# Loading four more input pieces before the first output store of a store-bound kernel

## The chip, the cores and the metric

The kernel runs on one core of one Trainium2 chip. The metric is the time of one execution on the device in microseconds (us), the median of several runs. The engines are named as in the profile. In that of the kernel before, PE runs the matrix products and transposes (2304 instructions), DVE, ACT and POOL the copies and casts (384, 481 and 106, a few other instructions of ACT and POOL among them), SP and ACT issue the transfers, and the DMA engines, of which the profile counts sixteen, carry them. SBUF and PSUM are the two memories that the program places its tiles in. Kernels are compared only within the same rounds.

## The reference

```python
# q, k: 8 x 12 x 1024 x 64, float32
def reference(q, k):
    return np.einsum('bhid,bhjd->bhij', q, k).astype(np.float32)
```

These are 96 heads. Each takes 256 KB of q and 256 KB of k and gives a 1024 x 1024 float32 matrix of 4 MB. In all 50.33 MB are read and 402.65 MB are written.

## The kernel before

Blocks of heads go through these steps: a load of raw float32 pieces (four pieces a block: q and k, twice), a cast to float16 on POOL, a transpose on PE, a copy to SBUF on DVE, the score matmuls on PE, copies of eight 128 x 1024 tiles a head from PSUM on ACT (tiles 0, 2, 3, 5, 7) and DVE (tiles 1, 4, 6), and one store of 4 MB a head, issued by SP. Blocks 0 and 1 have two heads, all others four. The parts that matter here:

```python
in_pool = ctx.enter_context(tc.tile_pool(name="in_pool", bufs=8))    # raw pieces, 512 KB each
out_pool = ctx.enter_context(tc.tile_pool(name="out_pool", bufs=4))  # 4 MB each
...
    def scores(self, n, side):
        ...
        for t in range(NT):
            ps = po_pool.tile([P, S], F32, tag="po")      # three PSUM buffers
            ...                                           # two matmuls
            if t in (1, 4, 6):
                pin(nc.vector.tensor_copy(out=o_sb[:, t], in_=ps))
            else:
                pin(nc.scalar.copy(out=o_sb[:, t], in_=ps))
            if t in side:
                side[t]()
        pin(nc.sync.dma_start(out=..., in_=o_sb))         # the store
...
# first loads: blocks 0 to 2 into a free output buffer ("early"), block 3 into in_pool
for b in blocks[:3]:
    for n in range(4):
        ...
        b.load(n, (nc.sync, nc.scalar)[n % 2], piece)
for n in range(4):
    blocks[3].load(n, (nc.sync, nc.scalar)[n % 2])
...
stream = [(b, n) for b in blocks[4:] for n in range(4)]
...
        b.scores(n, side)
        if i == n == 0:
            next_load()          # after head 0: a pair of loads on ACT's queue
        next_load()              # after every head: one load on ACT's queue
        if nxt and a == nxt.G - 1 and 0 < i + 3 < len(blocks):
            to_half(blocks[i + 3 : i + 4])   # casts
```

So four of the eight input buffers stay empty at the start, and the first of them are filled by the pair that follows head 0. Every instruction is kept in program order on its engine. ACT both copies tiles and issues loads, and it does so in that order.

Of the kernel before, what the change touches and what calls it, by code (L numbers as in the profile page):

```python
# [15 lines left out]
def kernel(  # L16
# [6 lines left out]
    nc = tc.nc  # L23
# [118 lines left out]
    blocks, first = [], 0  # L142
# [10 lines left out]
    for b in blocks[:3]:  # L153
# [1 line left out]
            piece = raw[:, at + n * b.elems :][:, : b.elems]  # L155
            b.load(n, (nc.sync, nc.scalar)[n % 2], piece)
        at += 4 * b.elems
    for n in range(4):
        blocks[3].load(n, (nc.sync, nc.scalar)[n % 2])
    make_identity(nc, ident)  # L160

    def to_half(some):
        half_sb = half_pool.tile([P, 2 * half_elems], F16, tag="half")
        at = 0
        for b in some:
            b.place(half_sb, at)
            at += 2 * b.elems
            for n in range(4):
                b.cast(n)

    to_half(blocks[:2])
    to_half(blocks[2:3])



    stream = [(b, n) for b in blocks[4:] for n in range(4)]

    def next_load():
        if stream:
            b, n = stream.pop(0)  # L180
            b.load(n, nc.scalar)

    blocks[0].alloc()
    for x in range(2):
# [1 line left out]
    for i, b in enumerate(blocks):  # L186
        nxt = blocks[i + 1] if i + 1 < len(blocks) else None
        if nxt:
            nxt.alloc()
        heads = 2 * b.G  # L190
        for n in range(heads):
            a = n - max(0, heads - 1 - nxt.G) if nxt else -1
            side = {}
            if nxt and 0 <= a < nxt.G:
                side = {
                    1: lambda: nxt.transpose(a, 0),
                    6: lambda: nxt.transpose(a, 1),
                }
            b.scores(n, side)
            if i == n == 0:  # L200
                next_load()
            next_load()
            if nxt and a == nxt.G - 1 and 0 < i + 3 < len(blocks):
                to_half(blocks[i + 3 : i + 4])


# [28 lines left out]
```

## Time and profile before

| | before |
|---|---|
| median of the first three runs | 1074.59 us |
| span of the profiled run | 1074.4 us |
| bytes moved by DMA | 453.42 MB, mean 422 GB/s |
| busy share of PE, ACT, DVE, POOL | 69%, 44%, 43%, 9% |
| chain that ended last | 79% DMA, stores landing |
| first store issued | 19.56 us |

The way to read it: the DMA engines are busy for 90% or more of every slice but the last, and they move 426 to 436 GB/s in every slice between the first and the last, while PE, the busiest compute engine, is between 40 and 90% in all but one of these (that one at 90% or more), so the time is the bytes over the rate, plus whatever time the DMA engines lose. I measure it with one figure, the **lag** at time t: t less the bytes moved until t over 431 GB/s. The bytes come from adding up the trace's packet records (a packet under way counts in proportion), so the lag is worked out and is not a view of the profile. It rises where the DMA engines stand idle or move less than 431 GB/s, and stays level where they run at that rate. It is a mean over the sixteen DMA engines. The prediction quotes the lines of before.

### The profile page before, as it was taken

Reading aid. Unit: us, or ns where it says so; the run is one execution under the profiler, and the core shown is the slowest. Engines: PE = TensorE matmul, PEld = TensorE weight load, DVE = VectorE, ACT = ScalarE, POOL = GpSimd, SP = SyncE. Lnnn points to the kernel's source line nnn. Section 1 sums busy time; section 2 is a strip of 40 time slices with the busy share of each in tenths; the row PEclk is TensorE's granted clock in tenths of the full one; section 3 lists DMA queues with packets and bytes.
Section 4 is the critical chain, followed back from the end, with each engine's and each line's share of the span. In section 5 each row is a group of like instructions: output and inputs, shape, how many; then the busy total and the mean of one; then the engine's idle time right before and its main releaser. Section 6 shows DMA issues by size and latency. Waiting matters only on the chain.

```text
span 1074.4 us, 6393 instructions
## 1 busy us (share of the span) xinstructions
PE 743.6 (69%) x2304; PEld 267.3 (25%) x2304; DVE 463.7 (43%) x384; ACT 477.2 (44%) x481; POOL 100.7 (9%) x106
## 2 busy tenths in 40 slices
PE   7977677676776757667676676767767676678740
PEld 2322222222222212222222222222222222223210
DVE  4645354452534535345353443434434444445420
ACT  4545444444444434444443544444444443544530
POOL 4100101010010100101010010100101010000000
PEclk9965555555555555555555555555555555555555
DMA  9999999999999999999999999999999999999993
GB/s 332 430 429 433 429 433 432 428 431 433 429 432 431 431 427 436 429 428 435 431 429 434 427 431 434 427 432 434 426 433 433 429 430 432 432 431 429 436 432 170
DMA packets 28257, 453.42 MB, mean 422 GB/s; under 512 B 3136, under 2 KB 3136, under 8 KB 15936
## 3 DMA queue, kind: packets, MB, share of 16 engines
q1 hardware_dynamic: 14976, 405.81, 87.7%
q10 hardware_dynamic: 13248, 47.19, 11.0%
q8 instruction: 18, 0.29, 0.1%
q14 instruction: 15, 0.12, 0.0%
HBM read 50.33 MB, written 402.65 MB: 422 GB/s over the span
## 4 chain that ended last, share of the span: by engine, by line
DMA 79%; PE 12%; ACT 4%; issue 0%; DVE 0%; ACTq 0%; POOL 0%; SPq 0%
DMA out_dram<-o_sb 79%; PE ps L128 12%; ACT o_sb L132 4%; PE t_ps L103 1%; DMA early<-in_q_dram 0%; DVE o_sb L130 0%; DVE kT L115 0%; ACTq L132 0%; POOL half_sb L88 0%; SPq L75 0%
## 5 line engine op out<-in xcount | busy, mean ns | idle before, releaser
L128 PE MATMUL ps<-kT,qT 64*128 64x512 f16 x1536 | 657.3, 621 | 289.8 <-ACT o_sb L132 286.4
L132 ACT COPY o_sb<-ps 128x1024 f32<-128x1024 f32 x480 | 475.9, 1013 | 554.7 <-DMA out_dram<-o_sb 347.6
L130 DVE COPY o_sb<-ps 128x1024 f32<-128x1024 f32 x288 | 352.7, 1225 | 568.9 <-DMA out_dram<-o_sb 404.5
L128 PEld LDWEIGHTS <-qT 64*128 64x128 f16 x1536 | 193.2, 134 | 687.0 <-issue 680.2
L88 POOL CAST half_sb<-x_sb 128x1024 f16<-128x1024 f32 x88 | 91.3, 1040 | 835.0 <-DMA x_sb<-in_k_dram 404.6
L103 PE MATMUL t_ps<-ident,half_sb 128*128 128x128 f16 x768 | 99.0, 310 | 6.1 <-POOL half_sb L88 6.1
L103 PEld LDWEIGHTS <-half_sb 128*128 128x128 f16 x768 | 74.1, 141 | 84.4 <-issue 62.4
L115 DVE COPY qT<-t_ps 128x1024 f16<-128x1024 f16 x48 | 60.6, 1263 | 7.2 <-PE t_ps L103 7.2
L115 DVE COPY kT<-t_ps 128x1024 f16<-128x1024 f16 x48 | 58.3, 1215 | 0.2 <-PE t_ps L103 0.2
L88 POOL CAST half_sb<-early 128x512 f16<-128x512 f32 (+1 forms) x12 | 8.7, 755 | 5.4 <-DMA early<-in_q_dram 5.4
L132 ACT ACT_TABLE_LOAD x1 | 1.3, 1283 | 8.8 <-DMA early<-in_q_dram 8.8
masks.py:199 POOL TENSOR_SCALAR_AFFINE_SELECT ident<-ident 128x128 f16<-128x128 f16 x1 | 0.3, 292 | 0.1
masks.py:197 POOL MEMSET ident<- 128x128 f16 x1 | 0.2, 204 | 0.3 <-POOLq L219 0.3
L219 POOL MEMSET const-float32-0.0<- 128x1 f32 x1 | 0.1, 98 | 0.2 <-issue 0.2
L219 POOL MEMSET const-bfloat16-1.0<- 128x1 bf16 x1 | 0.1, 101 | 0.0
L219 POOL MEMSET const-uint8-127<- 128x1 uint8 x1 | 0.1, 101 | 0.0
L219 POOL MEMSET const-float32-1.0<- 128x1 f32 x1 | 0.1, 98 | 0.0
## 6 DMA issues: line engine op xcount, KB each, us to landing
out_dram<-o_sb SPq DMA_DIRECT2D x96, 4096.0 KB, 36.7
x_sb<-in_k_dram ACTq DMA_DIRECT2D x44, 512.0 KB, 32.1
x_sb<-in_q_dram ACTq DMA_DIRECT2D x42, 512.0 KB, 32.1
early<-in_k_dram ACTq DMA_DIRECT2D x4, 256.0 KB, 5.0
early<-in_q_dram SPq DMA_DIRECT2D x4, 256.0 KB, 4.8
early<-in_q_dram SPq DMA_DIRECT2D x2, 512.0 KB, 7.3
early<-in_k_dram ACTq DMA_DIRECT2D x2, 512.0 KB, 7.4
x_sb<-in_q_dram SPq DMA_DIRECT2D x2, 512.0 KB, 9.3
```

The source lines that it names most:

```text
L88: nc.gpsimd.tensor_copy(out=self.halves[n % 2][:, :, n // 2], in_=self.raw[n].rearrange("p (r d) -> p r d", d=D),)
L103: pin(nc.tensor.transpose(t_ps[:, t], rows, ident))
L115: pin(nc.vector.tensor_copy(out=dst, in_=src))
L128: pin(nc.tensor.matmul(ps[:, js], qT[cs, g, t], kT[cs, g, js]))
L130: pin(nc.vector.tensor_copy(out=o_sb[:, t], in_=ps))
L132: pin(nc.scalar.copy(out=o_sb[:, t], in_=ps))
L219: nc = _bacc.Bacc("TRN2", target_bir_lowering=False, num_devices=1)
```

## The change

The intent is to fill all eight input buffers at the very start, where the DMA engines have nothing else to do (in the trace of before no load moves between 18.18 and 19.50 us, and no store yet), and from the second head on to load one piece a head, two heads ahead of the old order.

```diff
-    for n in range(4):
-        blocks[3].load(n, (nc.sync, nc.scalar)[n % 2])
+    stream = [(b, n) for b in blocks[3:] for n in range(4)]
+
+    def next_load(eng):
+        if stream:
+            b, n = stream.pop(0)
+            b.load(n, eng)
+
+    for n in range(8):
+        next_load((nc.sync, nc.scalar)[n % 2])
     make_identity(nc, ident)
 ...
-    stream = [(b, n) for b in blocks[4:] for n in range(4)]
-
-    def next_load(): ...
 ...
             b.scores(n, side)
-            if i == n == 0:
-                next_load()
-            next_load()
-            if nxt and a == nxt.G - 1 and 0 < i + 3 < len(blocks):
+            if nxt and a == nxt.G - 1 and i + 3 < len(blocks):
                 to_half(blocks[i + 3 : i + 4])
+            if i + n > 0:
+                next_load(nc.scalar)
```

More of the change, by code (lines that the diff above doesn't have):

```diff
@@ L172 @@
     to_half(blocks[2:3])
-    stream = [(b, n) for b in blocks[4:] for n in range(4)]
-    def next_load():
-        if stream:
-            b, n = stream.pop(0)
-            b.load(n, nc.scalar)
     blocks[0].alloc()
```

## The prediction

The "18 such packets" are those of the page's instruction queue (q8: 18 packets, 0.29 MB; q14: 0.12 MB); that they make the tail of 14 us is an estimate from these bytes and the 431 GB/s. So is the store's reading ahead of its first write, in the sum and in the rivals (a) and (d): its 1.8 us are the lag that the trace of before gains from 19.5 to 23.5 us, its 1.2 us are the 1.21 us that a 32 KB packet takes there, and no trace shows the reading. That each issue waits for the one four earlier on its queue is right for the fifth and sixth of each queue in that trace; the seventh and eighth waited for transfers of the other queue.

> **What bounds the kernel now.** I read the page first (slices, queues, chain of waits), then the windows view in steps of one microsecond over the first 45 us, then the windows over the last 44 us, and last the timelines of ACT and POOL over the first 20 us. The page says that the DMA engines are the bound, from end to end:
>
> ```profile
> PE   7977677676776757667676676767767676678740
> ...
> DMA  9999999999999999999999999999999999999993
> GB/s 332 430 429 433 429 433 432 428 431 433 429 432 431 431 427 436 429 428 435 431 429 434 427 431 434 427 432 434 426 433 433 429 430 432 432 431 429 436 432 170
> ...
> q1 hardware_dynamic: 14976, 405.81, 87.7%
> q10 hardware_dynamic: 13248, 47.19, 11.0%
> ...
> DMA 79%; PE 12%; ACT 4%; issue 0%; DVE 0%; ACTq 0%; POOL 0%; SPq 0%
> ```
>
> Every slice but the first and the last moves 426 to 436 GB/s with the DMA row full, while PE has idle time in each. The chain is 79% the landing of output stores: PE waits for ACT, ACT for an output buffer, the buffer for its store. The bytes are fixed: 453.42 MB at about 431 GB/s are 1052 us. Of the 1074.4 us only some 22 us can be won by a change in the order of transfers, and only where the DMA engines stand idle. The windows show the two such places. The first is the hand-over from the first loads to the first store (the last two columns are the DMA share and GB/s):
>
> ```profile
> 17.00:18.00 1.00, 1.00 (x9) 0.53 (x8) 1.00 (x2) 0.00 (x0) 0.34 (x1) 1.00 0.83 328
> 18.00:19.00 1.00, 1.00 (x6) 0.31 (x3) 0.95 (x1) 0.47 (x1) 1.00 (x2) 1.00 0.01 4
> 19.00:20.00 1.00, 0.76 (x3) 0.13 (x2) 0.61 (x1) 1.00 (x2) 1.00 (x2) 1.00 0.43 66
> 20.00:21.00 1.00, 0.93 (x3) 0.22 (x2) 0.61 (x1) 0.82 (x2) 1.00 (x2) 1.00 1.01 336
> 21.00:22.00 1.00, 1.00 (x4) 0.39 (x3) 0.00 (x0) 0.94 (x2) 0.65 (x1) 1.00 1.08 213
> 22.00:23.00 1.00, 1.00 (x4) 0.33 (x3) 0.44 (x1) 0.72 (x1) 0.00 (x0) 1.00 0.99 221
> ```
>
> The second is the end, from 1058 to 1072 us, with a DMA share near 0.06 (one engine of 16) and 16 to 33 GB/s: one engine finishes its part of the last store some 14 us after the other fifteen. That engine sets the end. The change does not touch what is on it.
>
> To weigh the first place I added up the packet records of the trace and took off what 431 GB/s would have needed, that is, the lag t - bytes(t)/431 GB/s: 3.0 us at t = 15, 3.2 at 17.8 (6.31 MB, all sixteen first loads), 4.8 at 19.5, 6.6 at 23.5, and then 6.65 to 6.9 us at every point up to 1055. So all that is ever lost at the front is lost before 24 us: 3.2 us by start-up and loads, 1.6 us in an empty hole (no packet at all from 18.16 to 19.48), and 1.8 us between 19.5 and 23.5, where the share is full but the loads that run there move only some 213 GB/s. [...]
>
> [...] The page of this trace has 18 such packets, 0.29 MB, and 0.12 MB on a second queue; 0.41 MB at 431/16 = 27 GB/s would be 15 us of one engine, which fits the 14 us tail if they all sit on one engine. That is an estimate; the change leaves it alone.
>
> **The change, part by part.** (1) It adds no bytes and no instructions: the same loads, four of them (2.10 MB) moved from heads 0 to 3 to the very start. (2) The four transfers come right behind the first sixteen, so they fill the hole. The sixteen moved 408 to 410 GB/s, so the last packet moves from 18.16 to about 18.16 + 2.10 MB / 409 GB/s = 23.3 us. (3) Later loads go out two heads earlier than before (after head h the piece that went out after head h+2). That ends POOL's 605 us of waiting for loads, but POOL is not on the chain. (4) The hidden cost is on ACT, whose sequencer takes issues and copies in order. The ACT timeline (start, duration):
>
> ```profile
> 4.37 0.33 ACTq L75 DMA_DIRECT2D early<-in_k_dram  x1
> ...
> 5.62 0.33 ACTq L75 DMA_DIRECT2D early<-in_k_dram  x1
> ...
> 8.42 0.33 ACTq L75 DMA_DIRECT2D x_sb<-in_k_dram  x1
> 8.78 1.28 ACT L132 ACT_TABLE_LOAD   x1 [8.78 <-DMA early<-in_q_dram]
> 10.39 1.01 ACT L132 COPY o_sb<-ps 128x1024 f32<-128x1024 f32 x1 [0.33 <-PE ps L128]
> 13.18 1.93 ACT L132 COPY o_sb<-ps 128x1024 f32<-128x1024 f32 x2 [1.77 <-PE ps L128]
> ...
> 18.53 1.01 ACT L132 COPY o_sb<-ps 128x1024 f32<-128x1024 f32 x1 [1.77 <-PE ps L128]
> ```
>
> The first four issues of each queue go out back to back; from the fifth on, each waits until the transfer four earlier on its queue has landed (SP's waits name the early tiles too). ACT's last new issue is its tenth, so it waits for its sixth, issued at 5.62. The landing of the early tiles is at most 8.1 us after the issue and POOL's cast of the last pieces starts at 13.45, so I take 13.6. Then: issue to 14.0, table load to 15.3, first copy at 15.3 instead of 10.39. PE may run ahead by three PSUM buffers (tiles 0 to 2); tile 3 needs the buffer of tile 0, so it starts at 15.3 + 1.05 = 16.4 instead of about 13.0. From there PE sets the pace as before, so head 0's last copy ends 3.4 us later, and its store is issued at 19.56 + 3.4 = 23.0 us.
>
> **The sum.** Before, loads end at 18.16 and the store's writes flow from about 23.5, with the lag settling at 6.65. After, loads end at 23.3 (8.40 MB, which at 431 GB/s are 19.5 us, a lag of 3.8 counted to the last packet's end). The store issued at 23.0 has its first activity 0.95 us later (as from 18.53 to 19.48), at 23.95, and must then read before its first writes: 1.8 us of lag before, or at least one 32 KB packet, 1.2 us. So writes flow from 25.1 to 25.7, with a lag of 25.1 - 19.5 = 5.6 to 6.2 us, middle 5.9. The gain is 6.65 - 5.9 = 0.8 us. The engine that finishes last stood in the same hole [...], so the gain goes through to the end: 1074.6 - 0.8 = 1073.8 us. Head 0's delay itself costs nothing more: stores follow each other every 7 to 9 us in that stretch (issues at 19.56, 26.16, 34.91, 43.05), faster than the 9.7 us that one needs on the DMA engines (4.19 MB / 431 GB/s), so the queue stays fed.
>
> **The rivals.** (a) ACT is not held: the wait that I put on its tenth issue is not there or ends early. Then store 0 goes out at 19.56, its reading lies beside the loads, the lag is 3.4 + 1.8 = 5.2 and the gain is 1.5 us: about 1073.1. For it: the waits view puts only SP's waits in this form. Against it: ACT's issues at 4.37, 5.62, 7.05 and 8.42 follow the same rhythm as SP's. (b) The wait takes the whole gain: store 0 is later than 23.0 (a later landing, a POOL cast or PE transpose that slips as well), at 25 us or more. Each microsecond past 23 is one of lag; the gain is gone at 23.8 and at 25 us the time is 1075.8. For it: the copies of head 0 are a chain over three PSUM buffers with little slack (PE is busy at 1.00 in nearly each of these windows). Against it: after tile 3 ACT and DVE have slack of 0.4 to 1.8 us a copy. (c) The earlier loads matter later: POOL's casts no longer wait, PE's 16 us of waiting for POOL go, and stores are ready earlier. For it: these waits are in the table. Against it: the DMA share is full in all those windows, so it is worth 0. Nor can it harm: the loads wait for a cast that in program order lies three heads before, so ACT is not held in the steady part. (d) All of the 3.4 us of hole and slow start is won: 1071.2. Against it: the store's reading has to come after its copies, and these come no earlier than before.
>
> **Range and chances.** The runs of before span 0.5 us. Rival (a) gives 1073.1, half of (b) 1074.9; with some room for another hand-over of the queues I take 1072.5 to 1075.2. A 2% change is 21 us, as much as all that is not steady transfer; I give 1 in 100 to each side.
>
> **What would show it.** In the changed profile: no empty window between 17 and 20 us, loads at 400 GB/s or more up to about 23; ACT's table load near 14 instead of 8.78 and its first copy near 15.3; the first store issued near 23.0 and a thin window at 23 to 25; all later slices at 431 GB/s as before; the one-engine tail of 14 us unchanged, ending about 1 us earlier; POOL's wait for loads almost gone and worth nothing. A table load at about 9 would make (a) right, a first store at 24 us or later (b), and a steady slice off 431 GB/s would mean that I had the bound wrong.

## The result, and the profile after

| | before | after |
|---|---|---|
| median of four runs | 1074.78 us (1074.47 to 1076.12) | 1072.37 us (1072.10 to 1073.12) |
| ratio, 95% interval | | 0.9976 (0.9959 to 0.9994) |
| span of the profiled run | 1074.4 us | 1070.7 us |
| first store issued | 19.56 us | 22.50 us |
| lag at 15, 25 and 60 us | 3.0, 6.7, 6.7 us | 3.3, 3.9, 4.2 us |

A ratio is the mean time of one kernel's runs over that of the other's of the same rounds, so it is not quite the ratio of the medians. The change gains 2.4 us, 0.24%. That is "the same" at a bar of 2%, but the interval excludes no gain. The time is 0.13 us below the range that was predicted, and the gain is three times the 0.8 us that the sum gave.

The page of the changed kernel, slices and chain:

```profile
DMA  9999999999999999999999999999999999999995
GB/s 372 429 432 428 434 425 438 426 432 432 425 432 429 431 432 426 433 429 428 434 426 431 425 435 425 432 427 432 423 435 422 433 422 423 431 432 430 435 432 243
...
DMA 75%; PE 13%; ACT 4%; issue 0%; ACTq 0%; SPq 0%
```

The first slice went from 332 to 372 GB/s; a slice is 26.8 us, so 40 GB/s more are 1.07 MB, or 2.5 us at 431 GB/s. The slices between the first and the last are at 422 to 438 GB/s, against 426 to 436 before: nothing was won there. Their mean even fell from 431.0 to 429.6, so more bytes were left for the last slice (243 GB/s against 170). What was won was won in the first 27 us.

The windows view of the changed kernel, one microsecond a row (last three columns: granted clock, DMA share, GB/s):

```profile
18.00:19.00 1.00, 1.00 (x4) 0.20 (x2) 0.93 (x1) 0.82 (x2) 0.00 (x0) 1.00 1.07 426
19.00:20.00 1.00, 1.00 (x8) 0.57 (x7) 0.46 (x1) 0.63 (x1) 0.00 (x0) 1.00 1.03 414
...
21.00:22.00 1.00, 1.00 (x6) 0.30 (x2) 0.89 (x1) 0.53 (x1) 1.00 (x2) 1.00 1.02 410
22.00:23.00 1.00, 0.76 (x3) 0.19 (x2) 0.67 (x1) 1.00 (x2) 1.00 (x2) 1.00 0.98 389
23.00:24.00 1.00, 1.00 (x4) 0.30 (x3) 0.55 (x1) 0.82 (x2) 1.00 (x2) 1.00 1.54 651
```

The hole of before (4 GB/s at 18 to 19) is gone, as foreseen. So is the slow stretch (213 and 221 GB/s at 21 to 23), which was not. The first 32 KB packet of the store is recorded at 23.35, 0.85 us after the issue, while the last loads are still ending. The thin window that I had foreseen at 23 to 25 is not there. The tail of one engine, foreseen as unchanged, is shorter: by the packet records one engine writes alone from 1062.3 to 1068.8 us, before from 1060.1 to 1072.4. (The 651 is a matter of counting: sixteen packets of 32 KB start within that microsecond, and a packet is counted where it starts.)

The timelines of ACT and SP in the changed kernel:

```profile
7.60 6.67 ACTq L75 DMA_DIRECT2D x_sb<-in_k_dram  x4
14.30 1.28 ACT L132 ACT_TABLE_LOAD   x1 [14.30 <-DMA early<-in_k_dram]
15.60 2.84 ACT L132 COPY o_sb<-ps 128x1024 f32<-128x1024 f32 x3
...
22.50 6.78 SPq L136 DMA_DIRECT2D out_dram<-o_sb  x2
```

ACT is held by its own issues until 14.3, 5.5 us longer than before (8.78), and store 0 goes out 2.9 us later. This part of the prediction held.

POOL's waits for loads, before and then after (the waits view; total us, times, longest us):

```profile
POOL half_sb L88 <- DMA x_sb<-in_k_dram: 404.6, 41, 10.6
POOL half_sb L88 <- DMA x_sb<-in_q_dram: 200.6, 20, 10.1
```

```profile
POOL half_sb L88 <- DMA x_sb<-in_k_dram: 197.4, 20, 10.0
POOL half_sb L88 <- DMA x_sb<-in_q_dram: 36.2, 19, 2.0
```

They fell from 605 to 234 us, less than I had thought, and POOL is not on the chain that ended last.

### The profile page after: what moved, and what is told of

Read it like the earlier page. It is cut to its first block, busy times and chain, and to the rows that moved or that the text cites. A ratio compares the mean times of both kernels' runs of the same rounds, so it can differ in the third digit from the quotient of the medians.

```text
span 1070.7 us, 6393 instructions
## 1 busy us (share of the span) xinstructions
PE 742.8 (69%) x2304; PEld 266.8 (25%) x2304; DVE 463.5 (43%) x384; ACT 476.8 (45%) x481; POOL 99.5 (9%) x106
## 4 chain that ended last, share of the span: by engine, by line
DMA 75%; PE 13%; ACT 4%; issue 0%; ACTq 0%; SPq 0%
DMA out_dram<-o_sb 72%; PE ps L128 11%; ACT o_sb L132 4%; DMA x_sb<-in_q_dram 3%; PE t_ps L103 2%; ACTq L132 0%; SPq L136 0%
## 5 line engine op out<-in xcount | busy, mean ns | idle before, releaser
L88 POOL CAST half_sb<-x_sb 128x1024 f16<-128x1024 f32 x88 | 90.0, 1040 | 816.1 <-PE t_ps L103 543.9
L132 ACT ACT_TABLE_LOAD x1 | 1.3, 1283 | 14.3 <-DMA early<-in_k_dram 14.3
```

The source lines that it names most:

```text
L88: nc.gpsimd.tensor_copy(out=self.halves[n % 2][:, :, n // 2], in_=self.raw[n].rearrange("p (r d) -> p r d", d=D),)
```

## The experiments

The open question was why the lag fell by 2.5 to 2.8 us (at 60 and at 25 us) instead of 0.8. The prediction had taken the slow stretch of 19.5 to 23.5 us for the store's own start and so for something that every order must pay. Twelve kernels were run, in four sets; in labels, b_ starts from the kernel before and a_ from the changed one. The table has all of them; lags are of the one profiled run of each. The diffs are shortened to their core.

| run | store 0 issued | lag at 15 / 25 / 60 us | median us | before, same rounds | ratio (95%) |
|---|---|---|---|---|---|
| b_again | 19.28 | 2.9 / 5.7 / 5.7 | 1075.20 | 1075.09 | 1.0004 (0.9990 to 1.0017) |
| a_again | 22.63 | 3.2 / 4.0 / 4.4 | 1072.46 | 1075.09 | 0.9978 (0.9966 to 0.9991) |
| b_pair_late | 19.73 | 3.1 / 5.9 / 7.9 | 1075.80 | 1075.56 | 1.0004 (0.9991 to 1.0016) |
| b_pair_sync | 19.37 | 2.8 / 5.6 / 7.5 | 1076.65 | 1075.09 | 1.0016 (1.0002 to 1.0030) |
| b_pair_early | 19.50 | 2.9 / 3.3 / 3.7 | 1072.39 | 1075.56 | 0.9972 (0.9960 to 0.9985) |
| b_store_wait | 22.74 | 3.0 / 6.5 / 6.9 | 1075.97 | 1076.00 | 1.0001 (0.9984 to 1.0017) |
| a_held_pair | 19.68 | 3.1 / 3.5 / 3.6 | 1072.59 | 1075.56 | 0.9973 (0.9960 to 0.9987) |
| a_old_pace | 22.06 | 3.0 / 3.5 / 3.8 | 1072.88 | 1075.56 | 0.9977 (0.9965 to 0.9990) |
| a_four_act | 19.43 | 2.9 / 3.3 / 3.3 | 1072.75 | 1075.09 | 0.9979 (0.9966 to 0.9991) |
| a_two_two | 19.49 | 2.9 / 4.5 / 4.5 | 1073.15 | 1076.00 | 0.9975 (0.9960 to 0.9989) |
| a_two_two_5 | 19.85 | 3.1 / 3.5 / 3.6 | 1072.51 | 1074.87 | 0.9972 (0.9956 to 0.9989) |
| a_tail_15 | 19.54 | 3.4 / 3.8 / 3.9 | 1092.02 | 1076.00 | 1.0150 (1.0134 to 1.0165) |

All results were correct.

### Does the store need its own start? b_pair_late

```diff
-            if i == n == 0:
-                next_load()
-            next_load()
+            if i == 0 and n == 1:
+                next_load(); next_load()
+            if i + n > 0:
+                next_load()
```

> The kernel before, with its two loads after head 0 issued after head 1 instead, so that nothing moves beside the first store. Collision theory: the 1.8 us of slow loads between 19.5 and 23.5 us come from the store waiting beside loads of the other queue, not from the store's own start; then the first 32 KB write is recorded 0.95 us after the issue at 19.56, near 20.5, the empty stretch grows to 2.3 us, the lag settles near 5.9 to 6.2 us (before: 6.7) and the time falls by about 0.5 to 0.8 us. Fixed-start theory (my prediction's): the store needs 1.8 us of reading before its first write whatever lies beside it; writes from about 22.3, lag near 7.7, time 1 us longer.

The windows of this run around the first store:

```profile
19.00:20.00 1.00, 0.76 (x3) 0.14 (x2) 0.56 (x2) 1.00 (x2) 1.00 (x2) 1.00 0.00 0
20.00:21.00 1.00, 1.00 (x3) 0.24 (x2) 0.78 (x1) 0.82 (x2) 1.00 (x2) 1.00 1.22 524
```

With no load beside it, the store issued at 19.73 has its first packet at 20.58, 0.85 us later, and all sixteen engines run at once (524 GB/s in the row from 20, that is, sixteen packets of 32 KB started in it). (The row from 19 shows the empty stretch.) The lag at 25 us is 5.9, as the collision theory said, and not 7.7. So the store has no start of 1.8 us: **the term of my sum is refuted.** The time did not fall, though. The lag rises again by 1.6 us between 50 and 60 us, and one of the waits of SP's queue in the first 70 us fits it:

```profile
SPq L136 <- DMA x_sb<-in_q_dram: 14.1, 1, 14.1
```

A store waited 14.1 us for a load, with which it shares nothing but a semaphore. By the trace it is number 102: the load's landing raised it at 53.74 and the store, the fourth, went out at 53.81. In the trace of before the fourth store went out at 43.05, and it was the sixth, issued at 62.64, that waited so, 11.7 us. Moving the pair moved which transfer follows which on the semaphores. The 0.8 us that the front had won over the first trace of before were lost there. Such waits of 8 to 13 us stand in other runs too (12.9 in b_again) and cost no lag that shows there.

### Does a load in flight slow down beside a store? a_held_pair, b_pair_early, a_old_pace

These ran with the one above. The first issues ACT's last two of the first eight loads from within head 0, after its tile 3:

```diff
     for n in range(8):
-        next_load((nc.sync, nc.scalar)[n % 2])
+        if n in (5, 7): held.append(stream.pop(0))
+        else: next_load((nc.sync, nc.scalar)[n % 2])
 ...
+            if i == n == 0:
+                side[3] = held_loads        # both on nc.scalar
             b.scores(n, side)
```

> The changed kernel, with ACT's last two of the eight first loads issued after its copy of tile 3 of head 0, so that ACT's copies are not held. Store 0 should again go out near 19.6 us, while loads of both queues flow until 23.3. Collision theory: from about 20.5 us the loads fall to some 213 GB/s, the lag settles at 5 to 5.5 us and the gain over before is 1.2 to 1.7 us, less than the changed kernel's 2.4, so the hold of ACT helps the changed kernel. Single-queue theory (loads are slow when one queue alone carries them): slow only where ACT's queue is alone, in the last 2 us. If neither, lag 4.0 and gain 2.4 or more.

The second leaves the kernel before as it is and only moves its pair from behind head 0 to behind tile 3 of head 0:

```diff
-            b.scores(n, side)
             if i == n == 0:
-                next_load()
-            next_load()
+                side[3] = lambda: (next_load(), next_load())
+            b.scores(n, side)
+            if i + n > 0:
+                next_load()
```

> The kernel before, with the pair of loads issued after ACT's copy of tile 3 of head 0 (near 14 us) instead of after the head. ACT's queue alone carries loads from 18.2 to about 20.7 us, and the store comes at 19.56. Collision theory: 400 GB/s until 20.3, hardly any overlap with the store, lag 4.0 to 4.4, gain over before 2.2 to 2.6 us without touching the other six of the change's moves. Single-queue theory: some 213 GB/s from 18.2 on, loads until 22.5 or later, lag 5.4 or more, gain about 1.2 us.

The third keeps the changed kernel's eight first loads and takes back the earlier later loads:

```diff
+            if i > 1 or (i == 1 and n == 1):
+                next_load(nc.scalar)
             if nxt and a == nxt.G - 1 and i + 3 < len(blocks):
                 to_half(blocks[i + 3 : i + 4])
-            if i + n > 0:
-                next_load(nc.scalar)
```

> The changed kernel's eight first loads, but later loads issued at the old pace (first one after head 3, before that head's casts), so two heads later than in the changed kernel. If all of the gain is made in the first 24 us: the same time as the changed kernel, 1072.4 us, lag 4.0 to 4.4. If the earlier later loads carry part of it: between the two, 1073 to 1074.5.

In a_held_pair the store was issued at 19.68 and loads ran on:

```profile
20.00:21.00 1.00, 1.00 (x3) 0.24 (x2) 1.00 (x1) 0.82 (x2) 1.00 (x2) 1.00 1.05 418
21.00:22.00 1.00, 1.00 (x4) 0.43 (x3) 0.12 (x1) 1.00 (x2) 0.77 (x1) 1.00 0.99 397
```

They moved 397 to 418 GB/s from 19 to 22 us: the collision theory, in the form in which I had put it, fell. In b_pair_early ACT's queue alone carried the loads at 401 GB/s from 18 to 19: the single-queue theory fell too, and moving two loads gave a gain as large as the whole change. a_old_pace gained 2.7 us in its rounds, so the earlier later loads are worth nothing that shows. And the hold of ACT costs nothing: without it (a_held_pair, 1072.59, ratio 0.9973) the time is that of the changed kernel (1072.46 on the same chip in the next set, ratio 0.9978).

### Is the slow stretch real, and is it the sharing? b_again, a_again, a_four_act, b_pair_sync

b_again and a_again are the two kernels with no edit, for a second trace of each. The first trace of before was of its slowest run.

> The kernel before, unchanged, for a second trace and the spread of its times, because its first trace was of its slowest run (1074.4 us of span against 1072.7 to 1074.0 in others). If the slow loads between 20.5 and 23.5 us belong to the kernel: again some 210 GB/s there and a lag of 6 to 6.8 us. If they were an accident of that one run: 400 GB/s, a lag near 5.2.

> The changed kernel, unchanged, on the same chip as the others: a lag of 3.6 to 4.4 us again, 1072.4 us, the store issued near 22 to 22.5 us with its first write 1 us later.

b_again has the same slow stretch in one of its rows:

```profile
20.00:21.00 1.00, 0.93 (x3) 0.25 (x2) 0.32 (x1) 0.82 (x2) 1.00 (x2) 1.00 1.01 369
21.00:22.00 1.00, 1.00 (x3) 0.30 (x2) 0.00 (x0) 0.93 (x2) 0.37 (x1) 1.00 1.07 250
```

It belongs to the kernel, but its size varies: from 19.5 to 25 us the lag rose by 1.0 us here and by 1.9 in the first trace. a_again repeated the changed kernel.

a_four_act leaves SP's queue empty and puts all four extra loads on ACT's, behind tile 3 of head 0:

```diff
-    for n in range(8):
+    for n in range(4):
         next_load((nc.sync, nc.scalar)[n % 2])
 ...
+            if i == n == 0:
+                side[3] = lambda: [next_load(nc.scalar) for _ in range(4)]
             b.scores(n, side)
```

> The changed kernel with all four loads of block 4 on ACT's queue, issued at once after ACT's copy of tile 3 of head 0 (near 14 us). SP's queue is then empty from 18 us, and the store (issued near 19.6) is at its head while ACT's queue still has loads until 23.3, as in the kernel before, but with no empty hole ahead and the loads' issue 4 us earlier. Theory A (a store at the head of its queue beside loads in flight on the other slows these to half and does not start itself): some 213 GB/s from 20.5 to about 25, lag 5 or more, gain over before 1.2 to 1.7 us. Theory B (the slow stretch of before is of loads issued just before the store, after an idle stretch, so tied to the issues and not to the sharing): 400 GB/s or more until 23.3, lag 3.6, gain 2.5 to 3 us.

```profile
20.00:21.00 1.00, 1.00 (x4) 0.24 (x2) 0.85 (x1) 0.82 (x2) 1.00 (x2) 1.00 1.02 410
21.00:22.00 1.00, 1.00 (x3) 0.29 (x2) 0.00 (x0) 1.00 (x2) 0.52 (x1) 1.00 1.00 393
```

The store was issued at 19.43, its own queue was empty, loads flowed on the other queue for three more microseconds, and they were not slowed. Theory A, the sharing itself, fell.

b_pair_sync puts the pair behind the store on SP's queue:

```diff
             if i == n == 0:
-                next_load()
-            next_load()
+                next_load(nc.sync); next_load(nc.sync)
+            else:
+                next_load()
```

> The kernel before, with the pair after head 0 issued on SP's queue behind store 0 instead of on ACT's queue before it; no other move, and the order of the semaphores stays (the run with the pair after head 1 lost its gain again at 52 to 57 us, where store 3 waited 14 us for a load's semaphore). Store 0 has the engines alone: first write 0.8 us after its issue, lag near 5.9 to 6.2 from 21 us on, gain over before 0.5 to 0.8 us. If the later loads or semaphores take it back, the lag will step up after 25 us.

The front did what was expected (lag 5.6 at 25 us), but another 1.9 us were lost between 25 and 40, and the kernel is 1.6 us slower than before. Two of its windows there:

```profile
29.00:30.00 1.00, 1.00 (x3) 0.30 (x2) 0.12 (x1) 1.00 (x2) 0.00 (x0) 1.00 0.00 0
...
33.00:34.00 1.00, 1.00 (x6) 0.15 (x2) 0.94 (x1) 0.48 (x1) 0.00 (x0) 1.00 1.08 266
```

The zero in the row from 29 is a matter of counting: no packet starts there, but the last sixteen packets of store 0, started between 28.5 and 29, still run. They took 1.96 us (median) in place of the usual 1.21 (medians of packet records; the usual one is that of before). From 28.5 to 31, where the loads take over from store 0, the lag rose by 0.8 us. From 31 to 36 it rose by 1.1 more, with the loads slow again at 33; the next store had been issued at 25.8 already and the one after it came at 34.55. So keeping the pair out of the first store's way is not enough, in this run, where it stands behind that store.

### Is it the empty stretch, or the nearness of the two issues? b_store_wait, a_two_two, a_two_two_5

What was left of the slow stretch's setting was that its loads follow an empty stretch, and that they are issued 1 us ahead of the store. b_store_wait keeps the empty stretch and puts the store off by 3 us, by three more copies of tile 7 (the same values) ahead of it:

```diff
+            if self.first + n == 0:
+                for _ in range(3):
+                    pin(nc.scalar.copy(out=o_sb[:, 7], in_=ps))
             pin(nc.sync.dma_start(...))          # the store
 ...
+            if i == n == 0:
+                side[7] = lambda: (next_load(), next_load())   # the pair, ahead of them
```

> The kernel before, with three more copies of tile 7 of head 0 (the same values again) between the issue of the pair of loads and the store, so that store 0 goes out near 22.5 us instead of 19.56; the empty hole stays. If the store's presence slows the loads that were issued just before it: now 350 to 400 GB/s from 20 to 22.4, and slow at no time; the lag then settles near 6 to 6.4, about as before, because the store comes later. If loads are slow after an empty stretch by themselves: again 210 to 250 GB/s from 20.5 us with no store issued, loads until 23 or later, lag 6.5 or more, time 0 to 0.7 us longer.

```profile
20.00:21.00 1.00, 0.29 (x1) 0.10 (x1) 0.65 (x1) 0.97 (x2) 1.00 (x2) 1.00 0.91 352
21.00:22.00 1.00, 0.71 (x2) 0.14 (x1) 0.00 (x0) 0.97 (x2) 0.69 (x1) 1.00 1.04 422
```

The same two loads, issued at 18.58 and 18.95 after the same empty stretch, ran at 422 GB/s and were through before 22.8. So in these traces the slow stretch came only with the store. It is not the whole rise, though: from the first load packet after the empty stretch the lag rose by 1.9 and 1.2 us in the two traces of before, and by 0.6 here without the store. Some 1.3 and 0.6 us are left for the store. The time is that of before because the store now came after a second hole (209 GB/s at 22 to 23).

a_two_two does the opposite: no empty stretch, but loads issued near the store.

```diff
-                side[3] = lambda: [next_load(nc.scalar) for _ in range(4)]
+                side[3] = lambda: [next_load(nc.scalar) for _ in range(2)]
+                side[7] = lambda: [next_load(nc.scalar) for _ in range(2)]
```

> As the run with four loads on ACT's queue, but only two of them issued after tile 3 of head 0 and the other two after its tile 7 (near 18.5 us), 1 us before the store, as in the kernel before; the first two fill the hole until about 20.7. If loads issued just before the store are slowed by it: 400 GB/s until about 20.7, then some 210 to 250 until 25, lag 4.5 to 5. If the slow stretch needs the empty hole ahead of it: 400 GB/s until 23.3, lag 3.4 to 3.6, the same time as with four at once, 2.3 us less than before.

```profile
19.00:20.00 1.00, 1.00 (x4) 0.34 (x3) 0.30 (x1) 1.00 (x2) 1.00 (x2) 1.00 1.05 422
...
21.00:22.00 1.00, 1.00 (x3) 0.37 (x3) 0.00 (x0) 0.58 (x1) 0.58 (x1) 1.00 1.00 307
22.00:23.00 1.00, 1.00 (x3) 0.30 (x2) 0.12 (x1) 0.98 (x1) 0.00 (x0) 1.00 1.06 213
```

The DMA engines were full all along (a share of 0.99 to 1.10 in the rows from 18 to 23), the last two loads were issued at 18.46 and 18.84 and the store at 19.49, and the loads fell to half the rate. The lag at 25 us is 4.5 against 3.3 with all four loads at 14 us. The last run moves the second two from tile 7 to tile 5 of head 0 (side[5]):

> As the run with two and two loads on ACT's queue, with the second two issued after tile 5 of head 0 (near 16.7 us, 2.8 us ahead of the store) instead of after tile 7 (18.5, 1 us ahead, where they fell to 213 to 307 GB/s and the lag went to 4.6). If only the nearness of the loads' issue to the store's matters: 400 GB/s until 23.3 and a lag of 3.4 to 3.6, as with all four at 14 us. If any load still in flight when the store is issued is slowed, unless it was issued some 5 us before: slow again, lag 4 or more. Time in either case 1072 to 1073.2, the difference within the spread.

```profile
21.00:22.00 1.00, 0.66 (x2) 0.24 (x2) 0.28 (x1) 0.00 (x0) 0.94 (x1) 1.00 1.01 401
22.00:23.00 1.00, 1.00 (x4) 0.29 (x3) 0.00 (x0) 0.62 (x1) 0.00 (x0) 1.00 1.46 598
```

Issued at 16.03 and 16.41, 3.4 to 3.8 us ahead of the store (19.85), they were not slowed, and the lag is 3.5. So in these traces **loads whose issue comes about 1 us ahead of the first store's are slowed, for one or two rows to about half, and the same loads issued 3.4 us or more ahead of it are not.** That rests on one profiled run of each kernel. The times do not tell the two apart: a_two_two has a ratio of 0.9975 and a_two_two_5 of 0.9972, with intervals of 0.0014 to 0.0017 to each side, and 1 us is 0.0009. What couples the loads and the store is not shown, and the nearness of the issues does not cover the slow loads of b_pair_sync, which were issued at 19.76 and 20.23, over 5 us ahead of the next store (25.80); a third load, on ACT's queue, was issued at 24.77. After the first heads the kernels issue a load about 1 us ahead of nearly each store while loads last (27.99 and 28.94 in the changed kernel; the usual gap is 0.98 us); what that costs where stores already fill the queue was not measured.

### A try at the tail: a_tail_15

```diff
+            last = self.first + n >= BH - 2
+            for ps in [slice(0, 120), slice(120, P)] if last else [slice(0, P)]:
+                pin(nc.sync.dma_start(out=to[ps], in_=got[ps]))
```

This starts from a_held_pair and has nothing to do with the change; it was a try at a kernel that beats both. The hope was that the cut stores take work off the one engine that ends last. How such stores are spread over the engines is shown by no trace of this case; what the expectation said of it is cut, and with it the grounds of its two answers, which stand as the author's estimates.

> The kernel with ACT's two held loads, and the last two heads' stores each cut into one of 120 partitions and one of 8, to learn whether the DMA engine that ends 14 us after the others is the last of the sixteen. [...] If the late one is the sixteenth, [...] the tail goes and the time falls by 8 to 12 us, to about 1061 to 1065. If it is another, [...] the time rises by 0 to 2.5 us.

```profile
1040.00:1050.00 10.00, 0.00 (x0) 0.00 (x0) 0.00 (x0) 0.00 (x0) 0.00 (x0) 0.50 0.86 252
```

It was 16 us slower than before, and before is itself some 3 us slower than a_held_pair in its rounds: outside of what either answer allowed. In this window of the cut stores 252 GB/s were moved; from 1040 to 1050 the changed kernel moved 436. The 32 KB packets took 1.8 to 1.9 us on average from 1040 to 1060 (packet records) instead of 1.21 (the median of before and of the changed kernel); why is not shown. Whether the late engine is the sixteenth can't be told from a run in which all of them were slowed.

## Why the prediction was wrong

**What bounds the kernel: right.** The DMA engines do. All runs but a_tail_15 can be read as bytes over rate plus lag: the time of each profiled run less its lag at 60 us is 1068.0 to 1069.5 us for both kernels and for each of these experiments. For example, a_two_two_5 has 1072.56 - 3.6 = 1069.0 and before has 1076.2 - 6.7 = 1069.5. The spread of 1.5 us is over half of the gain, so this reading is a rough one.

**The hole and its filling: right.** The lag rose by 1.6 us from 17.8 to 19.5 before and by 0.1 after. The last loads ended near 23.9, against 23.3 predicted.

**The hold of ACT: right in kind and nearly in size.** The table load came at 14.30 (predicted 14.0), the first copy at 15.60 (15.3), the store at 22.50 (23.0). The waits that I read from ACT's rhythm are real (its last issue went out at 13.94 and ended at 14.27), which decides against rival (a) as a description of this kernel, although its number, 1073.1, came nearest: luck. The reading was off in one point. Eight semaphores, 100 to 107 in the trace, go round over both queues, so that ACT's tenth issue waited for SP's sixth transfer (landed at 13.92 in the trace) and not for ACT's own sixth (14.25). But the hold is worth nothing either way: a_held_pair without it has the same time.

**The step that failed** is the one that said of the store, whose reading no trace shows, that it "must then read before its first writes: 1.8 us of lag before, or at least one 32 KB packet, 1.2 us". There is no such term. The first packet comes 0.85 us after the issue in the changed kernel and in b_pair_late alike, and that delay lies beside the last loads when the store is issued at 22.5 and the loads end near 23.9. I had added 0.95 + 1.2 to 1.8 us behind the loads and got a lag of 5.6 to 6.2; it was 3.9 and 4.0 in the two traces. The slow stretch of before that I had read as the store's start, 1.9 us of lag in one trace and 1.0 in the other, was a cost of the kernel before: its pair of loads came after an empty stretch and was issued 1 us ahead of the store. The change removed it by accident, because it has no load to issue near the first store.

**Rival (d)**, which gave 1071.2 for winning the whole hole and slow start, was nearer than my centre. What I held against it, that the store has to come after its copies, is so in the traces (in before the last copy of head 0 ends at 19.54 and the store is issued at 19.56) and costs nothing that shows.

**What the sum lacked on the other side:** the first loads of the changed kernel are themselves a little slower in its two traces. The lag at 15 us is 3.2 to 3.3 against 2.8 to 3.1 in the other runs. It need not be the change: a_tail_15, with the first loads of a_held_pair (3.1), has 3.4.

**Rival (c)** and its dismissal held: a_old_pace shows nothing for the earlier later loads that stands out of the spread. That POOL's waits would almost go was too much (605 to 234 us).

**What stays open.** In the first pair of traces the lag at 60 us fell by 2.5 us and the profiled runs differ by 3.7; in the second pair it fell by 1.3 and they differ by 1.8; the medians differ by 2.4 and 2.6. So 0.5 to 1.2 us of these differences lie in something that this lag does not see. Nor does the lag stay level in the steady part: at 1000 us it is 6.8 and 7.0 in the two traces of before, but 7.5 and 7.8 in those of the changed kernel, which ends earlier all the same, and 3.5 in a_held_pair, which is no faster than the changed kernel. So the mean over the engines does not set the end. The engine that ends last writes alone for 12.3 us in the first trace of before and for 6.5 us in that of the changed kernel, and I take it that what the others lose on the way has that much room. The trace names no engine, so that I could not follow the last one, and why the steady part differs is not known.

No version beat the changed kernel by more than the spread: those with a lag of 3.3 to 3.8 us at 60 us ran 1072.4 to 1072.9, the changed kernel 1072.4 to 1072.5. The smallest edit with the whole gain is b_pair_early, which moves only two loads of the kernel before.

## What to carry to other kernels

In a kernel that is bound by its stores, look at the hand-over from the first loads to the first store: fill it with loads that have a free buffer anyway, and, as far as one trace each can tell, issue them some microseconds ahead of that store (3.4 us: 401 GB/s, a_two_two_5) rather than just before it (1 us: 213 to 307 GB/s, a_two_two). A slow stretch beside an event in one trace isn't yet the cost of that event: measure the event with nothing beside it before its cost goes into a sum (here 0.85 us from issue to first packet, not 1.8). And moving a transfer also moves which transfers share a semaphore; a gain at the front can be lost to such a wait 30 us later (14.1 us of waiting and 1.6 us of lag in b_pair_late). And where one engine ends well after the others, a mean over all of them does not tell the end (at 1000 us the lag is 6.8 in before and 7.5 in the changed kernel, which ends 3.7 us earlier).
